# Attention scores on two halves of the array, with q and k transposed once

## The chip, the cores and the metric

The kernel is one layer of a streaming-encoder trunk. It runs on one core of a Trainium2 chip, in one launch. The metric is device time in microseconds, median of several runs.

The names used below: PE (TensorE) multiplies on a 128 x 128 array; "PEld" is its loading of weights (the stationary operand). DVE (VectorE), ACT (ScalarE) and POOL (GpSimd) work on rows of data; SP issues DMAs. A matmul contracts over the partitions of its two operands and writes to PSUM, of which this kernel's pool holds eight banks of 128 x 512 fp32.

## The reference, cut to what matters

```python
B_HEADS, B_HD, CHUNK, B_LEFT_CHUNKS = 8, 64, 64, 8      # SEQ = 1024, D_MODEL = 1024

def band_attention(q, k, v, qn_g, kn_g, rel_bias):
    """each chunk attends to itself and the previous 8 chunks"""
    qh = head_rms(q.reshape(bsz, seq, B_HEADS, B_HD), qn_g)
    kh = head_rms(k.reshape(bsz, seq, B_HEADS, B_HD), kn_g)
    ...
    scores = jnp.einsum('bnqhd,bnkhd->bnhqk', qc, kb) * (B_HD ** -0.5)
    scores = jnp.where(valid, scores + bias, -1e30)
    probs = jax.nn.softmax(scores, axis=-1)
    o = jnp.einsum('bnhqk,bnkhd->bnqhd', probs, vb)

def reference(...):
    h = rmsnorm(x, norm_mix_g)
    qa, fa, ia, ga, qb, kb, vb, gate_a, gate_b = jnp.split(h @ w_in, split_at, axis=-1)
    oa = hgrn2_mixer(qa, fa, ia, ga, ...)
    ob = band_attention(qb, kb, vb, ...)
    merged = sigmoid(gate_a) * (oa @ w_branch_a) + sigmoid(gate_b) * (ob @ w_branch_b)
    x = x + merged @ w_out
    ...     # then a SwiGLU feed-forward and a gated projection of p, each with its own rmsnorm
```

The change concerns the line of `scores`: per head, 128 queries at a time against up to 640 keys (five blocks of 128), over 64 channels.

## The kernel before

The kernel splits an fp32 operand into a high part rounded to fp32r and a residual ("hi" and "lo"), and computes hi x hi + hi x lo + lo x hi, each product in fp32r. The large products do so over 128 partitions.

The program runs in stages: the input projections (to 300 us of the profile), the recurrence `hgrn_mix` with further projections woven in (to about 432 us), the attention (432 to about 638 us), and then the branches, the output projection, the feed-forward and the last projection. Each engine executes its own queue in the order in which the Python code emits instructions. The helpers `self.V`, `self.A`, `self.mul`, `self.tr` and `self.load` pin that order on DVE, ACT, PE and SP; for that reason most instructions carry the line of the helper in the profile: L72 (DVE, ACT, POOL), L102 (matmul), L105 (transpose), L142 (the cast of a loaded weight to its high part).

**The attention stage.** `attention` walks through 32 steps. A step is a pair of heads and a block of 128 queries; two pairs alternate over the eight blocks (steps 0 to 15), then the two others do (16 to 31). In step n, in this order, with "feed" being a generator of other work for PE:

1. `stage(n-1, 1)`: DVE finishes the softmax of head 1 of the step before (reciprocal, scaling).
2. a feed call: two chunks of a projection, six 512-column products (in the first 28 steps `attn_in`, which makes q and k of the other head pairs; then the gates).
3. `scores(n, 0)`: head 0's score products, and DVE's reductions that add the bias and find the row maximum.
4. the first part of `attn_stack(n+1)`: transposes of the next q and k, and ACT's copies out of PSUM.
5. `scores(n, 1)`, then the rest of `attn_stack(n+1)` on DVE (the residuals).
6. in odd steps `attn_pv` of two earlier steps: probabilities times v, 40 records on PE, the two heads on the two column halves of the array.
7. `attn_pt(n-1, 1)`: five transposes of head 1's probabilities, copied out by ACT and DVE.
8. a second feed call.
9. `stage(n, 0)`, `stage(n, 1)`: ACT's exponentials; `attn_pt(n-1, 0)`; ACT's scaling of head 0; one queued residual split of weights on DVE (`rest`).

**The stack.** A head has 64 channels, half of the partitions. `attn_in` writes each head's q and k twice side by side (tile qk, the axis `two`), so that one transpose gives a 128-partition tile with the 64 channels twice. Of q the upper copy holds the high part and the lower copy the residual (`lo = qs[64:128, :]`); of k, `k1` holds the high part in both halves and `k2` the residual. Two products then give the sum: q with k1 (hi x hi + lo x hi) and q with k2. That takes four transposes and, per head, two products over 128 partitions; scores wider than 512 columns are cut in two parts, one PSUM bank each (384 + 256 columns for five key blocks). The tiles are named in the profile by role: m are small tiles (qk, qs, s, pt, bias, statistics), s are 128 x 1024 slots (k1, k2, v, activations), pm is PSUM, wh, wl and wr are a weight's high part, residual and raw load.

Of the kernel before, what the change touches and what calls it, by code (L numbers as in the profile page):

```python
# [22 lines left out]
HALF = 512  # L23
# [21 lines left out]
def f32(ap):  # L45
    return ap.bitcast(F32)
# [28 lines left out]
class Trunk:  # L75
# [526 lines left out]
                    self.nc.scalar.activation(self.v[p][:, b * P:b * P + P], ps[:, p * P:p * P + P], AF.Copy, scale=self.r[:, b:b + 1])  # L602

    def attn_setup(self):
        self.k1 = [self.slot(F32R) for _ in range(4)]
        self.k2 = [self.slot(F32R, late=i > 1) for i in range(4)]
        self.qs = {}

    def attn_in(self):

        nc = self.nc
        late = []

        def scale():
            two, b, ps, ss = late.pop(0)
            for i in range(2):
                qk = self.small(HALF, tag="qk")
                self.V.tensor_tensor(
                    qk[:, :].rearrange("p (a two d) -> p a two d", two=2, d=64),
                    ps[:, i * 256:i * 256 + 256].rearrange("p (a d) -> p a d", d=64).unsqueeze(2).to_broadcast([P, 4, 2, 64]),  # L620
                    ss[:, 4 * i:4 * i + 4].unsqueeze(2).unsqueeze(3).to_broadcast([P, 4, 2, 64]), ALU.mult)
# [24 lines left out]
    def attn_stack(self, pair, b):  # L646

        qk = self.qk.pop((pair, b))
        ps = self.mm()
        for a in range(4):  # L650
            self.tr(ps[:, a * P:a * P + P], qk[:, a * P:a * P + P], self.eye)
        t = slice(b * P, b * P + P)
        gk = self.cols[:, C_GK:C_GK + 1]
        k1, k2 = [k[pair % 2 * 2:pair % 2 * 2 + 2] for k in (self.k1, self.k2)]
        qs = self.small(256, F32R, tag="qs")
        self.qs[pair, b] = [qs[:, h * P:h * P + P] for h in range(2)]
        ksrc = [ps[:, 256 + h * P:256 + h * P + P] for h in range(2)]
        qsrc = ps[:, 0:256]
        self.A.activation(k1[0][:, t], ksrc[0], AF.Copy, scale=gk)
        self.A.activation(qs, qsrc, AF.Copy, scale=self.gq8[:, 0:1])  # L660
        self.A.activation(k1[1][:, t], ksrc[1], AF.Copy, scale=gk)
        yield
        lo = qs[64:128, :]
        for h in range(2):
            self.V.scalar_tensor_tensor(k2[h][:, t], ksrc[h], gk, f32(k1[h][:, t]), ALU.mult, ALU.subtract)
            if h == 0:
                self.V.scalar_tensor_tensor(lo, qsrc[64:128, :], self.gq8[64:128, 0:1], f32(lo), ALU.mult, ALU.subtract)

    def attn_scores(self, pair, b, h):

# [4 lines left out]
        bias = self.bias[pair, h]  # L675
        q = self.qs[pair, b][h]
        k1, k2 = [k[pair % 2 * 2 + h] for k in (self.k1, self.k2)]
        s = self.small(640, tag="s")
        mx = self.small(2, tag="mx2")
        last = None  # L680
        for i, (lo, hi) in enumerate(((0, na), (na, cols))):
            if hi == lo:
                continue
            ps = self.mm()
            n = hi - lo
            self.mul(ps[:, :n], q, k1[:, k0 + lo:k0 + hi], start=True, stop=False)
            self.mul(ps[:, :n], q, k2[:, k0 + lo:k0 + hi], start=False, stop=True)
            init = 3.0e38 if last is None else last
            self.V.tensor_tensor_reduce(s[:, lo:hi], ps[:, :n], bias[:, 640 - cols + lo:640 - cols + hi], -1.0, init, ALU.add, ALU.min, mx[:, i:i + 1])
            last = mx[:, i:i + 1]  # L690
        yield s, nb
        den = self.small(1, tag="den")
        self.A.activation(s[:, :cols], s[:, :cols], AF.Exp, bias=last, scale=-1.0, accum_out=den)
        yield
        self.V.reciprocal(den, den)
        if h == 0:
            self.A.activation(s[:, :cols], s[:, :cols], AF.Copy, scale=den)
        else:
            self.V.tensor_scalar(s[:, :cols], s[:, :cols], den, None, ALU.mult)

    def attn_pt(self, s, nb):
        pt = self.small(640, tag="pt")
# [19 lines left out]
    def attention(self):  # L722
# [17 lines left out]
        def scores(n, h):  # L740
            stages = self.attn_scores(*steps[n], h)
            sc[n, h] = (*next(stages), stages)

        def stage(n, h):
            if 0 <= n < whole:
# [19 lines left out]
        for n in range(whole + 2):  # L765
# [1340 lines left out]
MIXER = {"s": 3, "pt": 4, "bias": 4, "qk": 4, "qs": 2, "sq": 1, "state": 2}  # L2106


class Small:
# [140 lines left out]
```

## Time and profile before

| what | value |
|---|---|
| median of 3 runs | 1547.46 us (1546.5 to 1548.7) |
| the profiled execution | 1549.86 us, its span 1548.0 us |
| PE busy in the span | 1520.7 us (98%) |
| DVE, ACT, POOL busy | 1127.2, 670.7, 626.7 us |
| attention stage, 432 to 638 us: PE, DVE, ACT busy | 199.9, 158.8, 147.8 of 206.0 us |
| granted TensorE clock | 1.00 |

How the profile's lines are read: a row of a group names line, engine, operation, out<-in by the tiles' names, shapes, and xcount; then the busy time in us, the mean of one in ns, and the engine's idle time just before them with what ended it. A row of the timeline begins with start and duration in us; alike neighbours are merged into one row with their count. The shape 128*64 128x128 of a PE row means weights of 128 rows and 64 columns, and an output of 128 columns. Matmuls are pipelined: a record's duration is longer than the time for which it holds up the next one, so costs on PE are taken from start to start. The chain of waits follows the work that ended last back from the end.

### The profile page before, as it was taken

Reading aid. Unit: us, or ns where it says so; the run is one execution under the profiler, and the core shown is the slowest. Engines: PE = TensorE matmul, PEld = TensorE weight load, DVE = VectorE, ACT = ScalarE, POOL = GpSimd, SP = SyncE. Lnnn points to the kernel's source line nnn. Section 1 sums busy time; section 2 is a strip of 40 time slices with the busy share of each in tenths; the row PEclk is TensorE's granted clock in tenths of the full one; section 3 lists DMA queues with packets and bytes.
Section 4 is the critical chain, followed back from the end, with each engine's and each line's share of the span. In section 5 each row is a group of like instructions: output and inputs, shape, how many; then the busy total and the mean of one; then the engine's idle time right before and its main releaser. Section 6 shows DMA issues by size and latency. Waiting matters only on the chain.

```text
span 1548.0 us, 20662 instructions
## 1 busy us (share of the span) xinstructions
PE 1520.7 (98%) x7664; PEld 1266.2 (82%) x7664; DVE 1127.2 (73%) x1645; ACT 670.7 (43%) x1136; POOL 626.7 (40%) x349
## 2 busy tenths in 40 slices
PE   8999999999999999999999999999999999999998
PEld 6888888878788888788888788888888888888886
DVE  5787774776777778446888877777777767656678
ACT  6633333433377677421567222222222234456552
POOL 4233333010333222245212656665555545445546
PEclk9999999999999999999999999999999999999999
DMA  5544444898433443767346244443233288785425
GB/s 201 195 164 143 143 150 154 270 325 258 145 82 69 111 75 73 294 178 230 102 158 216 91 119 125 128 124 111 104 110 101 101 303 305 273 282 188 130 96 203
DMA packets 97044, 256.56 MB, mean 166 GB/s; under 512 B 10032, under 2 KB 14896, under 8 KB 96432
## 3 DMA queue, kind: packets, MB, share of 16 engines
q1 hardware_dynamic: 90400, 239.51, 45.0%
q0 software_dynamic: 6400, 15.73, 6.2%
q8 instruction: 60, 0.98, 0.3%
q14 instruction: 40, 0.33, 0.1%
q10 hardware_dynamic: 144, 0.02, 0.0%
HBM read 193.08 MB, written 93.59 MB: 185 GB/s over the span
## 4 chain that ended last, share of the span: by engine, by line
PE 89%; DVE 6%; ACT 2%; DMA 1%; issue 1%; POOL 0%; SPq 0%; DVEq 0%; ACTq 0%; POOLq 0%
PE pm L102 86%; DVE s L72 4%; PE pm L105 3%; DVE m L72 1%; ACT m L72 0%; ACT wh L142 0%; DMA s<-in_x 0%; DMA wr<-in_qk 0%; DMA wr<-in_fm 0%; DVE q L72 0%; ACT s L72 0%; DVE wl L72 0%; DMA wr<-in_wv 0%; DVE s L337 0%; DVE t L72 0%
## 5 line engine op out<-in xcount | busy, mean ns | idle before, releaser
L102 PE MATMUL pm<-s,whi 128*128 128x512 f32 x1792 | 552.4, 389 | 0.6 <-DVE t L72 0.6
L102 PE MATMUL pm<-s,wh 128*128 128x512 f32 (+1 forms) x1584 | 492.5, 392 | 7.0 <-ACT wh L142 5.2
L102 PEld LDWEIGHTS pm<-s,whi 128*128 128x128 f32 x1792 | 336.0, 188 | 71.5 <-DVE t L72 1.7
L102 PEld LDWEIGHTS pm<-s,wh 128*128 128x128 f32 x1584 | 295.6, 188 | 69.9 <-ACT wh L142 5.2
L102 PE MATMUL pm<-s,wlo 128*128 128x512 f32 x896 | 348.6, 389 | 0.0
L72 DVE TENSOR_TENSOR s<-s,s 128x512 f32<-128x512 f32 (+3 forms) x236 | 285.5, 1238 | 61.2 <-ACT s L72 47.7
L102 PE MATMUL pm<-s,wl 128*128 128x512 f32 x792 | 308.7, 390 | 0.5 <-POOL wl L150 0.5
L150 POOL TENSOR_TENSOR wl<-wr,wh 128x1024 fp32r<-128x1024 f32 (+2 forms) x72 | 175.3, 2440 | 222.5 <-ACT wh L142 222.4
L72 DVE TENSOR_TENSOR t<-pm,t 128x512 f32<-128x512 f32 x158 | 108.8, 689 | 132.9 <-PE pm L102 105.6
L142 ACT CAST wh<-wr 128x1024 fp32r<-128x1024 f32 (+2 forms) x106 | 106.5, 1005 | 208.4 <-PE pm L102 92.1
L102 PEld LDWEIGHTS pm<-s,wlo 128*128 128x128 f32 x896 | 168.2, 188 | 34.8
L102 PE MATMUL pm<-wh,s 128*128 128x512 f32 x512 | 180.0, 407 | 0.0
L102 PEld LDWEIGHTS pm<-s,wl 128*128 128x128 f32 x792 | 149.2, 188 | 32.0 <-POOL wl L150 1.2
L72 POOL TENSOR_TENSOR wlo<-wr,whi 128x512 fp32r<-128x512 f32 (+1 forms) x63 | 132.3, 2106 | 68.2 <-ACT whi L72 59.2
L72 POOL TENSOR_TENSOR wlo<-q,whi 128x512 fp32r<-128x512 f32 x62 | 100.0, 1614 | 139.7 <-ACT whi L72 75.5
L72 POOL TENSOR_TENSOR m<-m,mhalf 128x8 f32<-128x8 f32 (+1 forms) x24 | 35.0, 1459 | 229.1 <-DVE m L72 229.1
L72 ACT CAST s<-s 128x1024 fp32r<-128x1024 f32 (+1 forms) x94 | 90.4, 981 | 61.9 <-DVE s L72 31.6
L72 ACT CAST whi<-q 128x512 fp32r<-128x512 f32 (+1 forms) x93 | 70.5, 758 | 107.3 <-PE pm L102 84.6
L102 PEld LDWEIGHTS pm<-wh,s 128*128 128x128 f32 x512 | 96.4, 188 | 18.5
L72 POOL TENSOR_TENSOR s<-t,rb 128x512 f32<-128x512 f32 x44 | 70.7, 1607 | 98.5 <-ACT t L72 96.1
L102 PE MATMUL pm<-wl,s 128*128 128x512 f32 x256 | 99.9, 390 | 0.0
L72 ACT ACTIVATE t<-s 128x512 f32<-128x512 f32 x44 | 27.8, 633 | 159.3 <-DVE s L72 155.3
(147 smaller groups left out, 1835.3 us busy)
## 6 DMA issues: line engine op xcount, KB each, us to landing
s<-d SPq DMA_DIRECT2D x81, 512.0 KB, 6.2
d<-s SPq DMA_DIRECT2D x87, 256.0 KB, 2.4
wr<-d SPq DMA_DIRECT2D x36, 512.0 KB, 3.7
d<-s SPq DMA_DIRECT2D x32, 512.0 KB, 4.4
d<-t SPq DMA_DIRECT2D x46, 256.0 KB, 2.3
wr<-in_sg SPq DMA_DIRECT2D x22, 512.0 KB, 3.9
wr<-in_su SPq DMA_DIRECT2D x22, 512.0 KB, 4.9
s<-in_x SPq DMA_DIRECT2D x21, 512.0 KB, 8.6
```

The lines of the kernel that those rows point to most:

```text
L72: return lambda *a, **k: self.trunk.order(op(*a, **k), self.key)
L102: return self.order(self.nc.tensor.matmul(*a, **k))
L105: return self.order(self.nc.tensor.transpose(*a, **k))
L142: self.nc.scalar.copy(hi[:, c], raw[:, c])
L150: rest.tensor_tensor(lo[:, c], raw[:, c], f32(hi[:, c]), ALU.subtract)
```

## The change

The two heads of a pair are no longer stacked. One transpose turns both heads' q (64 channels each, 128 together) and one both heads' k. `q1`, `k1` are the high parts and `q2`, `k2` the residuals, in tiles that hold head 0 in partitions 0 to 63 and head 1 in 64 to 127. Each head's scores are now three products over its own 64 partitions; the products of the two heads are written in turn, and each goes to the half of the array's rows on which its operands lie. They write to different PSUM banks.

Around it: `attn_in` writes q and k once (one DVE operation of 512 columns per block instead of two); the stack issues two ACT copies and two DVE residuals instead of three and three; both heads' score products stand together, ahead of the next step's stack; head 1's row of scores takes a slot of the pool late1; the squares of `attn_in` share the buffers of qk; and the second feed call moves from behind `attn_pt(n-1, 1)` to ahead of `attn_pv`.

```diff
     def attn_setup(self):
-        self.k1 = [self.slot(F32R) for _ in range(4)]
-        self.k2 = [self.slot(F32R, late=i > 1) for i in range(4)]
+        self.ks = [[self.slot(F32R) for _ in range(2)] for _ in range(2)]
...
         def scale():
             two, b, ps, ss = late.pop(0)
+            qk = self.small(HALF, tag="qk")
+            self.V.tensor_tensor(
+                qk[:, :].rearrange("p (a d) -> p a d", d=64), ps[:, :].rearrange("p (a d) -> p a d", d=64),
+                ss[:, :].unsqueeze(2).to_broadcast([P, 8, 64]), ALU.mult)
             for i in range(2):
-                qk = self.small(HALF, tag="qk")
-                self.V.tensor_tensor(
...
-                self.qk[2 * two + i, b] = qk
+                self.qk[2 * two + i, b] = qk[:, 256 * i:256 * i + 256]
...
-                sq = self.small(HALF, tag="sq")
+                sq = self.small(HALF, tag="qk")
...
     def attn_stack(self, pair, b):
-        for a in range(4):
+        for a in range(2):
             self.tr(ps[:, a * P:a * P + P], qk[:, a * P:a * P + P], self.eye)
...
+        k1, k2 = self.ks[pair % 2]
         qs = self.small(256, F32R, tag="qs")
-        self.A.activation(k1[0][:, t], ksrc[0], AF.Copy, scale=gk)
-        self.A.activation(qs, qsrc, AF.Copy, scale=self.gq8[:, 0:1])
-        self.A.activation(k1[1][:, t], ksrc[1], AF.Copy, scale=gk)
+        q1, q2 = self.qs[pair, b] = qs[:, :P], qs[:, P:]
+        self.A.activation(k1[:, t], ps[:, P:2 * P], AF.Copy, scale=gk)
+        self.A.activation(q1, ps[:, :P], AF.Copy, scale=self.gq8[:, 0:1])
         yield
-        lo = qs[64:128, :]
-        for h in range(2):
-            self.V.scalar_tensor_tensor(k2[h][:, t], ksrc[h], gk, f32(k1[h][:, t]), ALU.mult, ALU.subtract)
-            if h == 0:
-                self.V.scalar_tensor_tensor(lo, qsrc[64:128, :], self.gq8[64:128, 0:1], f32(lo), ALU.mult, ALU.subtract)
+        self.V.scalar_tensor_tensor(k2[:, t], ps[:, P:2 * P], gk, f32(k1[:, t]), ALU.mult, ALU.subtract)
+        self.V.scalar_tensor_tensor(q2, ps[:, :P], self.gq8[:, 0:1], f32(q1), ALU.mult, ALU.subtract)

-    def attn_scores(self, pair, b, h):
+    def attn_scores(self, pair, b):
...
-            self.mul(ps[:, :n], q, k1[:, k0 + lo:k0 + hi], start=True, stop=False)
-            self.mul(ps[:, :n], q, k2[:, k0 + lo:k0 + hi], start=False, stop=True)
+        banks = [[self.mm() for _ in parts] for _ in range(2)]
+        for i, (lo, hi) in enumerate(parts):
+            c = slice(k0 + lo, k0 + hi)
+            for j, (q, k) in enumerate(((q1, k1), (q1, k2), (q2, k1))):
+                for h in range(2):
+                    r = slice(64 * h, 64 * h + 64)
+                    self.mul(banks[h][i][:, :hi - lo], q[r, :], k[r, c], start=j == 0, stop=j == 2)
+
+        def softmax(h):
...
+            s = self.slot(late=True)[:, :640] if h else self.small(640, tag="s")
...
     def attention(self):
...
-                scores(n, 0)
-            st = stack(n + 1)
-            next(st, None)
-            if n < whole:
-                scores(n, 1)
-            drain(st)
+                scores(n)
+            drain(stack(n + 1))
+            next(feed, None)
             if n % 2:
                 pv(n - 3)
                 pv(n - 2)
             pt(n - 1, 1)
-            next(feed, None)
             stage(n, 0)
```

What this does to the queues, in one odd step with five key blocks. On PE, before, from the first feed call's last product to the start of `attn_pv` (s_3771 and s_3772 are the k1 tiles of the two heads, s_3775 and s_3776 their k2, m_4788 is the q tile qs, m_4815 the next qk, m_4752 the transposed probabilities, s_2891 is v):

```order
L102 MATMUL pm_4766<-wh_4659,s_185 128x512
L102 MATMUL pm_4852<-s_3771,m_4788 128x384
L102 MATMUL pm_4852<-s_3775,m_4788 128x384
L102 MATMUL pm_4856<-s_3771,m_4788 128x256
L102 MATMUL pm_4856<-s_3775,m_4788 128x256
L105 MATMUL pm_4860<-eye,m_4815 128x128 x4
L102 MATMUL pm_4871<-s_3772,m_4788 128x384
L102 MATMUL pm_4871<-s_3776,m_4788 128x384
L102 MATMUL pm_4875<-s_3772,m_4788 128x256
L102 MATMUL pm_4875<-s_3776,m_4788 128x256
L102 MATMUL pm_4882<-m_4752,s_2891 64x128
```

The same place after the change (s_3768 is k1 and s_3769 k2, both heads in each; pm_4811 and pm_4812 are head 0's banks, pm_4813 and pm_4814 head 1's; the rows of the third product, which name the same tiles as the first, and those of the second part but its first are left out):

```order
L102 MATMUL pm_4729<-wh_4622,s_185 128x512
L102 MATMUL pm_4811<-s_3768,m_4763 128x384
L102 MATMUL pm_4813<-s_3768,m_4763 128x384
L102 MATMUL pm_4811<-s_3769,m_4763 128x384
L102 MATMUL pm_4813<-s_3769,m_4763 128x384
...
L102 MATMUL pm_4812<-s_3768,m_4763 128x256
...
L105 MATMUL pm_4835<-eye,m_4768 128x128 x2
L102 MATMUL pm_4729<-wh_4666,s_192 128x512
...
L102 MATMUL pm_4855<-m_4715,s_2888 64x128
```

Twelve score products stand where eight stood, in pairs; two transposes where four stood; and a feed call (its first product is shown) is between the stack and `attn_pv`.

On ACT, before, in the step in which a weight's cast (L142) is the feed's (s_3857 and s_3913 are outputs of `attn_pv`, m_4720 is the transposed probabilities, m_4664 and m_4683 are the score rows whose exponentials are taken):

```order
L72 COPY s_3857<-pm_4696 128x128
L72 COPY s_3913<-pm_4708 128x128
L72 COPY m_4720<-pm_4721 128x384
L142 CAST wh_4737<-wr_4738 128x1024
L72 ACTIVATE m_4742<-pm_4562 128x512
L72 ACTIVATE m_4664,m_4748<-m_4664,m_4665 128x640
L72 ACTIVATE m_4683,m_4750<-m_4683,m_4684 128x640
```

And after the change:

```order
L142 CAST wh_4666<-wr_4667 128x1024
L72 ACTIVATE m_4671<-pm_4527 128x512
L72 COPY s_3844<-pm_4677 128x128
L72 COPY s_3896<-pm_4689 128x128
L72 COPY m_4701<-pm_4702 128x384
L72 ACTIVATE m_4643,m_4711<-m_4643,m_4644 128x640
L72 ACTIVATE s_4647,m_4713<-s_4647,m_4648 128x640
```

The feed's cast and its square now stand ahead of the copies of `attn_pv`'s outputs and of the probabilities.

More of the change, by code (lines that the diff above doesn't have):

```diff
@@ L615, in scale @@
             two, b, ps, ss = late.pop(0)
+            qk = self.small(HALF, tag="qk")
+            self.V.tensor_tensor(
+                qk[:, :].rearrange("p (a d) -> p a d", d=64), ps[:, :].rearrange("p (a d) -> p a d", d=64),
+                ss[:, :].unsqueeze(2).to_broadcast([P, 8, 64]), ALU.mult)
             for i in range(2):
-                qk = self.small(HALF, tag="qk")
-                self.V.tensor_tensor(
-                    qk[:, :].rearrange("p (a two d) -> p a two d", two=2, d=64),
-                    ps[:, i * 256:i * 256 + 256].rearrange("p (a d) -> p a d", d=64).unsqueeze(2).to_broadcast([P, 4, 2, 64]),
-                    ss[:, 4 * i:4 * i + 4].unsqueeze(2).unsqueeze(3).to_broadcast([P, 4, 2, 64]), ALU.mult)
-                self.qk[2 * two + i, b] = qk
+                self.qk[2 * two + i, b] = qk[:, 256 * i:256 * i + 256]
         for two in range(2):
@@ L653, in attn_stack @@
         gk = self.cols[:, C_GK:C_GK + 1]
-        k1, k2 = [k[pair % 2 * 2:pair % 2 * 2 + 2] for k in (self.k1, self.k2)]
+        k1, k2 = self.ks[pair % 2]
         qs = self.small(256, F32R, tag="qs")
-        self.qs[pair, b] = [qs[:, h * P:h * P + P] for h in range(2)]
-        ksrc = [ps[:, 256 + h * P:256 + h * P + P] for h in range(2)]
-        qsrc = ps[:, 0:256]
-        self.A.activation(k1[0][:, t], ksrc[0], AF.Copy, scale=gk)
-        self.A.activation(qs, qsrc, AF.Copy, scale=self.gq8[:, 0:1])
-        self.A.activation(k1[1][:, t], ksrc[1], AF.Copy, scale=gk)
-        yield
-        lo = qs[64:128, :]
-        for h in range(2):
-            self.V.scalar_tensor_tensor(k2[h][:, t], ksrc[h], gk, f32(k1[h][:, t]), ALU.mult, ALU.subtract)
-            if h == 0:
-                self.V.scalar_tensor_tensor(lo, qsrc[64:128, :], self.gq8[64:128, 0:1], f32(lo), ALU.mult, ALU.subtract)
-    def attn_scores(self, pair, b, h):
+        q1, q2 = self.qs[pair, b] = qs[:, :P], qs[:, P:]
+        self.A.activation(k1[:, t], ps[:, P:2 * P], AF.Copy, scale=gk)
+        self.A.activation(q1, ps[:, :P], AF.Copy, scale=self.gq8[:, 0:1])
+        yield
+        self.V.scalar_tensor_tensor(k2[:, t], ps[:, P:2 * P], gk, f32(k1[:, t]), ALU.mult, ALU.subtract)
+        self.V.scalar_tensor_tensor(q2, ps[:, :P], self.gq8[:, 0:1], f32(q1), ALU.mult, ALU.subtract)
+    def attn_scores(self, pair, b):
         nb = min(b + 1, 5)
@@ L674, in attn_scores @@
         na = {1: 1, 2: 2, 3: 3, 4: 2, 5: 3}[nb] * P
[L675 to L685, printed above, removed]
-            self.mul(ps[:, :n], q, k1[:, k0 + lo:k0 + hi], start=True, stop=False)
-            self.mul(ps[:, :n], q, k2[:, k0 + lo:k0 + hi], start=False, stop=True)
-            init = 3.0e38 if last is None else last
-            self.V.tensor_tensor_reduce(s[:, lo:hi], ps[:, :n], bias[:, 640 - cols + lo:640 - cols + hi], -1.0, init, ALU.add, ALU.min, mx[:, i:i + 1])
-            last = mx[:, i:i + 1]
@@ L691, in attn_scores @@
[L691 to L699, printed above, removed]
+        q1, q2 = self.qs.pop((pair, b))
+        k1, k2 = self.ks[pair % 2]
+        parts = [(lo, hi) for lo, hi in ((0, na), (na, cols)) if hi > lo]
@@ new lines, in attn_scores @@
+        banks = [[self.mm() for _ in parts] for _ in range(2)]
[6 more added lines that the diff above has]
+        def softmax(h):
+            bias = self.bias[pair, h]
+            s = self.slot(late=True)[:, :640] if h else self.small(640, tag="s")
+            mx = self.small(2, tag="mx2")
+            last = None
+            for i, (lo, hi) in enumerate(parts):
+                init = 3.0e38 if last is None else last
+                self.V.tensor_tensor_reduce(
+                    s[:, lo:hi], banks[h][i][:, :hi - lo], bias[:, 640 - cols + lo:640 - cols + hi], -1.0, init, ALU.add, ALU.min, mx[:, i:i + 1])
+                last = mx[:, i:i + 1]
+            yield s, nb
+            den = self.small(1, tag="den")
+            self.A.activation(s[:, :cols], s[:, :cols], AF.Exp, bias=last, scale=-1.0, accum_out=den)
+            yield
+            self.V.reciprocal(den, den)
+            if h == 0:
+                self.A.activation(s[:, :cols], s[:, :cols], AF.Copy, scale=den)
+            else:
+                self.V.tensor_scalar(s[:, :cols], s[:, :cols], den, None, ALU.mult)
@@ L701, in attn_pt @@
+        return [softmax(h) for h in range(2)]
     def attn_pt(self, s, nb):
@@ L738, in stack, with scores @@
             return self.attn_stack(p, b)
-        def scores(n, h):
-            stages = self.attn_scores(*steps[n], h)
-            sc[n, h] = (*next(stages), stages)
+        def scores(n):
+            for h, stages in enumerate(self.attn_scores(*steps[n])):
+                sc[n, h] = (*next(stages), stages)
         def stage(n, h):
@@ L2105 @@
 FFN = {"q1024": 1, "q512": 3, "raw": 2, "tmp": 8}
-MIXER = {"s": 3, "pt": 4, "bias": 4, "qk": 4, "qs": 2, "sq": 1, "state": 2}
+MIXER = {"s": 3, "pt": 4, "bias": 4, "qk": 4, "qs": 2, "state": 2}
 class Small:
```

## The prediction

> **What bounds the kernel now.** I read the page first, then the stretches of the attention stage, the groups inside it, PE's rows in order of time, and last the chain of waits.
>
> ```profile
> PE 1520.7 (98%) x7664; PEld 1266.2 (82%) x7664; DVE 1127.2 (73%) x1645; ACT 670.7 (43%) x1136; POOL 626.7 (40%) x349
> PE 89%; DVE 6%; ACT 2%; DMA 1%; issue 1%; POOL 0%; SPq 0%; DVEq 0%; ACTq 0%; POOLq 0%
> ```
>
> PE is busy 98% of the span and is 89% of the chain that ended last. The attention stage, from 432 to 638 us, looks the same:
>
> ```profile
> core 0: us, PE busy (x) PEld busy (x) DVE busy (x) ACT busy (x) POOL busy (x), PEclk, DMA share, GB/s
> 432.00:638.00 206.00, 199.89 (x1486) 173.10 (x1485) 158.80 (x510) 147.75 (x381) 56.91 (x38) 1.00 0.41 96
> ```
>
> PE 97%, DVE 77%, ACT 72%, granted clock 1.00. So a ns saved or added on PE here is a ns of the end, unless a wait swallows it. What one step costs PE is read from one step, n=15, and the start of the next (five key blocks; start, time, engine, out<-in, count). A record lasts longer than its turn on the array, so I use start to start:
>
> ```profile
> 521.31 0.76 PE L102 MATMUL pm<-s,m 128*128 128x384 f32 x4
> 521.91 0.60 PE L105 MATMUL pm<-eye,m 128*128 128x128 f32 x4
> 522.26 0.84 PE L102 MATMUL pm<-s,m 128*128 128x384 f32 x4
> 523.03 2.40 PE L102 MATMUL pm<-m,s 128*64 128x128 f32 x40
> 525.37 0.77 PE L105 MATMUL pm<-eye,m 128*128 128x128 f32 x5
> 525.89 0.47 PE L102 MATMUL pm<-wh,s 128*128 128x512 f32 x1
> 527.36 0.71 PE L105 MATMUL pm<-eye,m 128*128 128x128 f32 x5
> 527.82 0.47 PE L102 MATMUL pm<-wh,s 128*128 128x512 f32 x1
> ```
>
> In order: the scores of head 0, the stack's transposes, the scores of head 1, the probabilities times v (attn_pv, two heads on the two column halves of the array), and the transposes of the probabilities.
>
> **The change, part by part.**
>
> *Transposes, four to two per step.* 32 steps lose 64 of them.
>
> ```profile
> 508.59 0.44 PE pm L105 x4
> ```
>
> That is 0.11 us each on the chain, so 64 x 0.11 = **-7.0 us**.
>
> *Score products, two per head to three, two heads at once.* Head 0 above streams 2 x (384 + 256) = 1280 columns from 521.31 to 521.91: 0.60 us, or 0.469 ns a column. The stage streams 80 x 384 + 112 x 256 + 16 x 128 = 61440 columns (the first two groups are the second and third row below, the rest the four steps with a single block):
>
> ```profile
> L105 PE MATMUL pm<-eye,m 128*128 128x128 f32 x376 | 57.9, 276 | 3.8 <-DVE m L72 3.8
> L102 PE MATMUL pm<-s,m 128*128 128x384 f32 x80 | 22.1, 357 | 0.0
> L102 PE MATMUL pm<-s,m 128*128 128x256 f32 x112 | 21.9, 289 | 2.3 <-DVE m L72 2.3
> L102 PE MATMUL pm<-m,s 128*64 128x128 f32 x480 | 29.7, 276 | 0.0
> ```
>
> 61440 x 0.469 ns = 28.8 us now. Afterwards each head streams three products instead of two, 92160 columns together. If the two heads run at once PE pays for 46080: 21.6 us, and some 0.6 us more because in the four one-block steps (three pairs each) a load of weights is longer than 128 columns. If they run one after the other it is 43.2 us. No product on part of the rows is in this trace; the nearest row is attn_pv, on part of the columns. Its 40 records take 523.03 to 525.37, 2.34 us; at 0.11 us each, as the transposes of the same 128x128 size, they would take 4.4 us in turn and 2.2 us in pairs. They run in pairs, and both ends stand: 22.2 us if rows pair as columns do, 43.2 us if they don't. I take pairs, the nearest row: 22.2 - 28.8 = **-6.6 us** (the other end: +14.4).
>
> *Changes of the array's mode.* Every step now leaves the full array for two row halves and comes back. The trace has the like around attn_pv. Going in: head 1's scores start at 522.26 and attn_pv at 523.03, 0.77 us for what took head 0 0.60; 0.08 of the difference was handed over by the transposes ahead (four in 0.35 instead of 0.44), so 0.09 is a wait. Within attn_pv: 2.34 - 20 pairs x 0.11 = 0.16, the first bare weight load and the wait at the way out. Coming back: five transposes take 525.37 to 525.89, 0.52, against 527.36 to 527.82, 0.46: 0.06 for their bare weight load. One round trip: 0.09 + 0.16 + 0.06 = 0.31 us. The scores' weights are fp32r, whose bare load is dearer; the last attn_pv goes back into such products:
>
> ```profile
> 631.16 2.40 PE L102 MATMUL pm<-m,s 128*64 128x128 f32 x40
> 633.50 0.72 PE L102 MATMUL pm<-s,wh 128*128 128x512 f32 x2
> 634.06 0.40 PE L102 MATMUL pm<-s,wl 128*128 128x512 f32 x1
> 634.30 0.62 PE L102 MATMUL pm<-s,wh 128*128 128x512 f32 x2
> 634.76 0.39 PE L102 MATMUL pm<-s,wl 128*128 128x512 f32 x1
> ```
>
> Two products take 0.56 (633.50 to 634.06) against 0.46 (634.30 to 634.76): 0.10 instead of 0.06, so a round trip for the scores is 0.31 + 0.05 = 0.36 us. All 32 steps make one, none shared with attn_pv's, since a feed call stands between: 32 x 0.36 = **+11.5 us**. The ends are 0 (halving rows costs nothing) and 32 x 0.6, were both ways to pay two fp32r loads in turn: +19.
>
> *Feed moved ahead of attn_pv and the transposes of head 1's probabilities.* The same instructions, earlier in five queues. On PE its six products (525.89 to 527.36 above less the 0.08, 1.39 us) now stand between the scores and whatever waits for the softmax; they cover PE's waits of this kind:
>
> ```profile
> 529.84 0.42 PE L102 MATMUL pm<-s,m 128*128 128x128 f32 x2
> 530.80 0.74 PE L105 MATMUL pm<-eye,m 128*128 128x128 f32 x5 [0.55 <-DVE m L72]
> 624.01 0.40 PE L102 MATMUL pm<-s,wl 128*128 128x512 f32 x1
> 627.16 0.74 PE L105 MATMUL pm<-eye,m 128*128 128x128 f32 x5 [2.76 <-DVE m L72]
> ```
>
> The first has head 1's probability transposes right behind the scores, waiting for DVE's normalisation: it starts 0.96 us after the products, of which about 0.2 is their own time, so some 0.75 go. The second waits for DVE, which sits in one residual split of weights:
>
> ```profile
> 623.51 2.85 DVE L72 TENSOR_TENSOR wl<-wr,wh 128x512 fp32r<-128x512 f32 x1
> 626.47 0.55 DVE L72 TENSOR_SCALAR m<-m,m 128x640 f32<-128x640 f32 x1
> ```
>
> The cover shortens it by 1.39 of its 2.76. The third long wait is a load's:
>
> ```profile
> 490.29 0.95 ACT wh L142
> 491.31 2.39 POOL wl L72
> 493.71 5.34 DMA wr<-in_qk
> 499.14 1.05 ACT wh L142
> ```
>
> ACT's cast waits for a load that waits for POOL's split of the cast before. In ACT's queue the earlier cast stands now ahead of a probability copy (0.48, row below) and has a k copy (0.36) less in front of it, so the load lands up to 0.8 us earlier; but ACT, blocked, now holds attn_pv's copies and head 1's probability copy too, which PE's next scores need for their banks. I take 0.4 off. Sum: -0.75 - 1.39 - 0.4 = **-2.5 us**. Ends: -5, if all waits of the stage that DVE ends go (PE's 3.8 before transposes and 2.3 before products, in the group rows above, less 1 that the load keeps), and +2, if the load's block costs a wait for banks of the same size as the 2.3 again. SP and POOL issue the same instructions in the same order, so the weight loads, the bias tables' loads and POOL's powers move past nothing in their own queues.
>
> *DVE and ACT.* The first five rows shrink:
>
> ```profile
> L72 ACT ACTIVATE s<-pm,cols 128x128 fp32r<-128x128 f32 x64 | 23.2, 363 | 3.0 <-PE pm L105 2.2
> L72 DVE SCALAR_TENSOR_TENSOR s<-pm,cols,s 128x128 fp32r<-128x128 f32 x64 | 22.4, 349 | 1.8 <-ACT s L72 0.7
> L72 DVE TENSOR_TENSOR m<-pm,m 128x512 f32<-128x512 f32 x30 | 19.2, 679 | 0.0
> L72 DVE SCALAR_TENSOR_TENSOR m<-pm,ones,m 64x256 fp32r<-64x256 f32 x32 | 15.7, 491 | 0.5
> L72 ACT ACTIVATE m<-pm,ones 128x256 fp32r<-128x256 f32 x32 | 14.9, 467 | 0.0
> L72 ACT COPY m<-pm 128x384 f32<-128x384 f32 x48 | 22.9, 477 | 6.4 <-PE pm L105 6.3
> L72 DVE CUSTOM_DVE_ANT_0 m<-pm,m 128x384 f32<-128x384 f32 x40 | 22.1, 553 | 16.8 <-PE pm L105 16.7
> L72 DVE CUSTOM_DVE_ANT_0 m<-pm,m,m 128x256 f32<-128x256 f32 x40 | 19.4, 484 | 3.6
> ```
>
> ACT loses 32 x 0.36 and 32 x (0.47 - 0.36), 15 us; DVE loses 32 x 0.35, 32 x (0.49 - 0.35) and 15 x 0.68, 26 us. Both hide under PE, so I count nothing. They are slack for the new order, in which DVE's four score reductions wait until the first part of both heads is through and q2 and k2 stand behind all four: 2 x 0.55 + 2 x 0.48 = 2.1 us of reductions (last two rows) and 2 x 0.35 for the two, 2.8 us, against the 4.1 that PE has until the next scores in a step without attn_pv (two feeds, 2.8, and twelve transposes, 1.3). If that cover went, each of the 32 steps would pay what is missing. Four banks are taken at once instead of two, but each step still takes the same number of the eight. The squares of attn_in share the four buffers of qk, of which each block again takes two, and head 1's score row moves into two buffers that held k; both cost nothing for the same reason, PE's cover.
>
> **Sum.** -7.0 - 6.6 + 11.5 - 2.5 = -4.6 us. The profiled execution took 1549.86 us (span 1548.0); that gives 1545.3. The runs' median, 1547.46, lies 2.4 lower, and the prediction is made for it: 1542.9.
>
> **Rivals.** A: *the two row halves run one after the other* (slower). Then the scores cost +14.4 instead of -6.6: 1542.9 + 21.0 = 1563.9. For it: nothing in the trace runs on half the rows. Against: the column halves pair. It decides from the pair's own price: with 1542.9 - 1547.5 = -4.6, a pair that takes 21% more than one product (4.6 of 22.2) brings no gain.
>
> B: *pairs, but dearer ones.* In attn_pv two loads of 0.05 fit under one product, so it can't show whether loads pair. Two fp32r loads of 0.10 in turn would give 0.2 us a pair; 156 pairs (3 x 20, 3 x 28, 3 x 4) make 31.2 instead of 22.2: +9.0, 1551.9. Milder: pairs at 1.3 of one product, 28.9, +6.7, 1549.6, no change or just slower. The Trainium skill ("TensorE: Matmul & The Clock Gate", Part 3, measured speedup) gives 3.07 for four row tiles of 32, 77% of the ideal; as an estimate from that, two tiles reach 1.54, a pair 1.3 of one product. No run here shows it; attn_pv's pairs at 1.0 speak against it.
>
> C: *halving the rows needs no change of mode.* Then the 11.5 us aren't paid: 1531.4. Against: both column modes pay at each change. The Trainium skill ("TensorEngine Tiling (Array Packing)", Key Properties) says that any change of tiling mode drains the array, by which C is out; the 0.31 us agree for columns, and no run here shows it for rows.
>
> D: *new waits eat the gain*: the banks and the blocked ACT above, +2 to +7 on the sum: 1545 to 1550.
>
> **How the numbers follow.** A measurement of this kernel can't tell less than about 0.2%, 3.1 us, from no change. The forecast has 0.53, its own range 1539 to 1547 (the pair's and the round trip's rounding, the waits' ends); about 0.40 of it is faster, 0.13 within. A 0.13, slower. B 0.14, half within and half slower. C 0.10, faster. D 0.10, mostly within. Together: faster 0.50, same 0.28, slower 0.22. The range takes in C at its low end and B at its high end and leaves out A: 1531 to 1556.
>
> **What would show it.** Right: the stage's transposes by 64 fewer; score records of 64 rows whose second head starts a few ns after the first, pairs at 0.18 (384 columns) and 0.12 (256); about 0.09 and 0.10 of idle around each group; no wait before head 1's probability transposes at the change from the first two head pairs to the next. Wrong: the second head's product a full product's time behind the first (A), pairs above 0.2 at 256 columns (B), no gap at the first score product (C), or waits of PE on DVE or ACT before the score products (D).

## The result, and the profile after

The changed kernel takes 1538.94 us (median of 4 runs, 1538.07 to 1539.85), the kernel before, beside it, 1547.01 us (1546.5 to 1548.7, 4 runs). The ratio is 0.9946, its 95% interval 0.9929 to 0.9963: 8.4 us faster, between 5.7 and 11.0. The forecast was 4.6 us faster. The profiled execution took 1538.07 us, its span 1536.3.

The page after: busy time by engine, and the chain that ended last by engine.

```profile
PE 1515.4 (99%) x7704; PEld 1248.4 (81%) x7704; DVE 1102.7 (72%) x1597; ACT 660.7 (43%) x1104; POOL 630.1 (41%) x349
PE 91%; DVE 5%; issue 1%; ACT 1%; DMA 1%; POOL 0%; SPq 0%; ACTq 0%; DVEq 0%; POOLq 0%
```

The stretch of the attention stage, which now ends some 10 us earlier, 2 of them for a wait of 2.06 us ahead of the stage, at 340.8 us, that this execution does not have (columns as in the prediction's row of 432 to 638 us):

```profile
432.00:626.00 194.00, 193.20 (x1511) 153.66 (x1509) 135.69 (x461) 137.34 (x348) 56.70 (x38) 1.00 0.42 100
```

PE is still the bound, at the same granted clock, and executes 40 instructions more (7664 before): 104 score products more, 64 transposes fewer. In the stage it is busy 193.2 of 194 us; before it was idle 6.1 of 206. The groups of the stage that changed, with the idle time ahead of them:

```profile
L105 PE MATMUL pm<-eye,m 128*128 128x128 f32 x182 | 31.9, 282 | 0.0
L105 PE MATMUL pm<-eye,s 128*128 128x128 f32 x120 | 19.2, 280 | 0.0
L102 PE MATMUL pm<-s,m 64*128 64x384 f32 x120 | 15.8, 368 | 0.0
L102 PE MATMUL pm<-s,m 64*128 64x256 f32 x168 | 15.1, 289 | 0.8 <-DVE m L72 0.8
L102 PE MATMUL pm<-s,m 64*128 64x128 f32 x24 | 2.2, 289 | 0.0
```

The 3.8 us of idle ahead of the transposes are gone, and of the 2.3 ahead of the 256-column products 0.8 are left. PE in order of time around one step's scores:

```profile
514.61 0.39 PE L102 MATMUL pm<-wh,s 128*128 128x512 f32 x1
514.93 1.16 PE L102 MATMUL pm<-s,m 64*128 64x384 f32 x12
516.02 0.44 PE L105 MATMUL pm<-eye,m 128*128 128x128 f32 x2
516.21 0.48 PE L102 MATMUL pm<-wh,s 128*128 128x512 f32 x1
516.52 0.40 PE L102 MATMUL pm<-wl,s 128*128 128x512 f32 x1
```

Twelve products stand between 514.93 and 516.02, 1.09 us. Two stretches of the timeline of a few ns show that they run in pairs; the first row has all that is in flight at 514.94, the second all by 515.22.

```profile
514.93 0.44 PE L102 MATMUL pm<-s,m 64*128 64x384 f32 x2
514.93 0.61 PE L102 MATMUL pm<-s,m 64*128 64x384 f32 x4
```

The second head's record starts 3 to 4 ns behind the first's (514.930 and 514.933, 515.209 and 515.213); the later pairs follow every 0.17 to 0.18 us at 384 columns and every 0.12 at 256. That is the price of one full-array product of the same width. The round trip shows too: the last product ahead of the group takes 0.327 (the median of the 32 groups; 0.32 here, 514.61 to 514.93) instead of 0.231, so 0.096 going in; the group takes 1.088 where six pairs at 0.177 and 0.118 take 0.885, so 0.203 for the bare load and the way out; the first transpose takes 0.165 instead of 0.109, so 0.056. Together 0.355 us.

### The profile page after: what moved, and what is told of

The parts are those of the page before. It is cut to its first block, busy times and chain, and to the rows that moved or that the text cites. A ratio compares the mean times of both kernels' runs of the same rounds, so it can differ in the third digit from the quotient of the medians.

```text
span 1536.3 us, 20676 instructions
## 1 busy us (share of the span) xinstructions
PE 1515.4 (99%) x7704; PEld 1248.4 (81%) x7704; DVE 1102.7 (72%) x1597; ACT 660.7 (43%) x1104; POOL 630.1 (41%) x349
## 4 chain that ended last, share of the span: by engine, by line
PE 91%; DVE 5%; issue 1%; ACT 1%; DMA 1%; POOL 0%; SPq 0%; ACTq 0%; DVEq 0%; POOLq 0%
PE pm L102 88%; DVE s L72 4%; PE pm L105 3%; DVE m L72 0%; DMA s<-in_x 0%; ACT s L72 0%; DVE q L72 0%; POOL wl L72 0%; DMA wr<-in_qk 0%; ACT m L72 0%; DVE s L337 0%; ACT wh L142 0%; DVE wlo L72 0%; DVE s L234 0%; ACT t L72 0%
## 5 line engine op out<-in xcount | busy, mean ns | idle before, releaser
L142 ACT CAST wh<-wr 128x1024 fp32r<-128x1024 f32 (+2 forms) x106 | 106.5, 1006 | 213.6 <-PE pm L102 94.3
```

The costliest lines, as they stand in the source:

```text
L142: self.nc.scalar.copy(hi[:, c], raw[:, c])
```

## The experiments

All ratios are to the kernel before, measured on the same chip at the same time. The name in brackets behind a heading is the label by which later paragraphs and the table call the run.

**The kernel before, again** (before_again). No edit.

> The kernel before, unchanged, as a control. The trace after lacks three waits of PE that the trace before had: 2.06 us at 340.8, 2.3 us at 500.4 and 2.76 us at 624.0. Theory 1 (chance of meeting): the first and the third arise when a DVE operation starts just after one of POOL's weight splits (2.4 us) and is held until that ends (2.85 us instead of 0.69); whether they meet depends on when a load lands, so they come and go between executions of the same program. Then this second profile lacks at least one of the two, and its span lies nearer the median of the runs (span 1544 to 1546). Theory 2 (fixed by the order): the waits belong to the program's order; then this profile shows all three within 0.3 us of the first and a span of 1548. Time for both: 1546 to 1549, ratio 1.000 within 0.15%.

1548.91 us, ratio 1.0002 [0.9993, 1.0010]. The wait of 2.06 us at 340.8 us, outside the change, which the first profile had, is absent; those at 498, 500, 528 and 622 us are all there, the first with 1.8 instead of 2.3 us and with a stretch of 3.4 us at half the granted clock behind it, from 501.3 us on. So the waits in attention belong to the order, and the 2 us at 340.8 (most of the gap between the profiled execution and the median, which the prediction subtracted) come and go; the second profile of the changed kernel has them.

**The feed call alone** (feed_only), moved in the kernel before:

```diff
             drain(st)
+            next(feed, None)
             if n % 2:
...
             pt(n - 1, 1)
-            next(feed, None)
```

> The kernel before with one edit: the second feed call stands ahead of attn_pv and of head 1's probability transposes. Scores and transposes are as before. Theory 2 (the cover of the feed removes the attention's waits, some 6 us): -5 to -6 us, 1541 to 1542. Theory 1 (the cover removes only what it covers, 0.75 + 0.4 + 0.4 + up to 1.4, the rest of the missing waits are chance meetings of DVE and POOL): -2 to -3 us, 1544 to 1545. Rival (the moved feed gains nothing by itself): 1547 within 1.

1556.1 us, ratio 1.0048 [1.0036, 1.0060]: 7.4 us slower. What PE waited for in its attention stage (430 to 640 us; time, times, longest):

```profile
PE pm L105 <- DVE m L72: 3.7, 10, 1.1
PE pm L105 <- ACT s L72: 1.1, 2, 0.6
PE pm L102 <- DVE m L72: 0.4, 2, 0.2
```

The waits are many and short; their sum, 5.2 us, is even below the 6.1 of the kernel before, and so does not explain the time. From its timeline, one of each kind, on PE and on DVE:

```profile
480.07 0.82 PE L102 MATMUL pm<-s,m 128*128 128x384 f32 x4
481.00 0.66 PE L105 MATMUL pm<-eye,m 128*128 128x128 f32 x4
...
501.26 0.77 PE L105 MATMUL pm<-eye,m 128*128 128x128 f32 x5 [0.49 <-ACT s L72]
...
500.81 0.56 DVE L72 CUSTOM_DVE_ANT_0 m<-pm,m 128x384 f32<-128x384 f32 x1 [2.66 <-PE pm L105]
```

The stack's transposes start 0.93 us after head 0's products instead of 0.60 (521.31 to 521.91 in the prediction). Taken from start to start, the loss shows. Here and below, PE's lost time is what its products take beyond the median for the same place in the order (the same kinds of products ahead and behind) over the traces of all runs, where that is over 0.06 us. It is 14.0 us in the stage, against 6.6 before, and the difference is the 7.4 us: 4.4 in 12 places ahead of the stack's transposes, 4.1 in 11 places at or behind the probability transposes, 3.9 in 33 places ahead of or among the score products, and 1.6 in two other places. The last row is head 1's first reduction on DVE: it waits for transposes of the step before, because its row of scores shares the three buffers s. The move puts a feed call in front of these transposes.

**The change without the feed call's move** (rows_only). In the changed kernel the call goes back behind `pt(n - 1, 1)`.

> The changed kernel with the second feed call put back behind head 1's probability transposes: only the scores on row halves and the two transposes are new. The array's terms as the prediction priced them give -7.0 - 6.6 + 11.5 = -2.1 us, so 1545 if the waits stay (theory 2: the cover was needed for them), with PE waiting about 1 us before head 1's probability transposes in short steps. Theory 1: -2 to -5 us, 1542 to 1545, as the meetings of DVE and POOL move with any change of timing. Rival (DVE's and ACT's relief removes the waits): 1539 to 1540, as the full change.

1542.4 us, ratio 0.9958 [0.9945, 0.9970]: 6.5 us faster, where the array's terms were to give 2.1. So the move, a loss by itself, would add some 2 us in the changed kernel, though the intervals of the two ratios overlap.

**attn_pv directly behind the scores** (pv_next), ahead of the stack and the feed call:

```diff
                 scores(n)
-            drain(stack(n + 1))
-            next(feed, None)
             if n % 2:
                 pv(n - 3)
                 pv(n - 2)
+            drain(stack(n + 1))
+            next(feed, None)
```

> The changed kernel with attn_pv moved ahead of the stack and the feed, directly behind the score products, so that in the 16 odd steps the array goes from row halves to column halves without the full array between. If each change of mode costs what the trace shows (0.10 us wait at the way out and 0.055 us for the bare load of the transposes' weights saved per odd step), 16 x 0.155 = -2.5 us against the changed kernel: 1536.5. If a change between two divided modes costs more than one to the full array, or attn_pv waits here for its probabilities' copies, no gain: 1539 or more.

1537.59 us, ratio 0.9932 [0.9919, 0.9946]. That is 1.5 to 2.2 us below the change by the ratios, but the intervals overlap: the 2.5 us are neither shown nor excluded.

**The changed kernel, again** (after_again), beside the next three.

> The changed kernel, unchanged, beside the others of this call on the same chip. Ratio to before 0.994 to 0.995 (1540 to 1541 where before takes 1549). Its trace has no wait of PE above 0.3 us in the attention but one of about 1 us at 496, and its attention stage takes 189.5 us for the products of before's 199 to 200.

1537.74 us, ratio 0.9942 [0.9928, 0.9956]. In attention its profile has one wait of PE, of 0.9 us, as expected.

**Head 0's products, then head 1's** (rows_serial), instead of in turn:

```diff
-            for j, (q, k) in enumerate(((q1, k1), (q1, k2), (q2, k1))):
-                for h in range(2):
+            for h in range(2):
+                for j, (q, k) in enumerate(((q1, k1), (q1, k2), (q2, k1))):
```

> The changed kernel with the score products in another order: head 0's three products of a part first, then head 1's, instead of in turn. Nothing else differs. If the array runs two row halves at once only where neighbours in the queue lie on different halves, three of four changes of half still pair and the rest run alone: per step with two parts of 384 and 256 columns 5 x 0.175 + 4 x 0.117 = 1.34 us instead of 0.88; over all steps +12 us. If order doesn't matter (the array looks ahead): 0. If pairs gave nothing in the first place: 0 as well, and the records of the changed kernel's pairs would not start 3 ns apart, which they do.

1539.45 us, ratio 0.9944 [0.9930, 0.9959]: no loss. The same cuts of the timeline, at 515.04, 515.05, 515.32 and 515.33, and the whole group:

```profile
515.04 0.44 PE L102 MATMUL pm<-s,m 64*128 64x384 f32 x1
515.04 0.45 PE L102 MATMUL pm<-s,m 64*128 64x384 f32 x2
515.04 0.61 PE L102 MATMUL pm<-s,m 64*128 64x384 f32 x3
515.04 0.62 PE L102 MATMUL pm<-s,m 64*128 64x384 f32 x4
...
515.04 1.16 PE L102 MATMUL pm<-s,m 64*128 64x384 f32 x12
```

Records start in pairs still, 10 ns apart instead of 3 (515.037 and 515.047, 515.316 and 515.326), and the group takes 1.094 us instead of 1.088. Three 384-column products in a row would take over 0.5 us before the other half's first could start; a second record starts 10 ns behind. The rows do not name the head, but products on the same half follow each other every 0.17 us, so the second record must be of the other half. PE thus starts head 1's first product, fourth in the program, ahead of head 0's second. The Trainium skill ("TensorE: Matmul & The Clock Gate", Part 3, The mechanism) says that matmuls start and end strictly in program order; read so, this trace disagrees, for products on different halves of the rows.

**Twenty more round trips** (extra_mode). The stack's two transposes go between the first and second part of the scores, in the 20 steps that have two parts:

```diff
+            if between is not None and i == 0 and len(parts) == 2:
+                next(between, None)
```

> The changed kernel with the next stack's two transposes set between the first and the second part of the score products, in the 20 steps that have two parts: 20 more round trips between the row halves and the full array, all else the same. By the price of 0.36 us a round trip: +7.2 us. If the round trip's gaps are hidden elsewhere (PE waits for DVE anyway): 0 to +2.

1546.3 us, ratio 0.9989 [0.9980, 0.9997]: 8.5 us above the changed kernel beside it. PE in order of time in one step:

```profile
483.02 0.40 PE L102 MATMUL pm<-wh,s 128*128 128x512 f32 x1
483.35 0.79 PE L102 MATMUL pm<-s,m 64*128 64x384 f32 x6
484.07 0.44 PE L105 MATMUL pm<-eye,m 128*128 128x128 f32 x2
484.44 0.63 PE L102 MATMUL pm<-s,m 64*128 64x256 f32 x6
485.00 0.50 PE L102 MATMUL pm<-wh,s 128*128 128x512 f32 x1
```

The two transposes take 0.37 us (484.07 to 484.44), where two at 0.11 make 0.22, and the bare load and the way out are paid in both parts. Attention, waits taken out, is 7.3 us longer: 0.37 us for each round trip, the prediction's 0.36. (8.5 us / 20 is 0.43.)

**DVE's relief given back** (dve_back). k2 and q2 are computed twice.

> The changed kernel with both residuals of a step (k2 and q2) computed twice: 32 x 0.70 = 22 us of DVE work back, near the 26 us that the change took off; results are the same. Theory 3 (the moved feed call only pays because DVE was relieved: with DVE's old load the back-to-back transposes wait for DVE's copies, which is what made the kernel with the feed call alone 7 us slower): +4 to +9 us, with PE waiting for DVE in many steps. Rival (what matters is the order of PE's own products; DVE is slack at 72% busy): 0 to +1 us.

1538.04 us, ratio 0.9940 [0.9928, 0.9952]: no change, with DVE up by 17 us (the page's busy times):

```profile
PE 1516.8 (99%) x7704; PEld 1250.0 (81%) x7704; DVE 1119.7 (73%) x1661; ACT 661.0 (43%) x1104; POOL 628.8 (41%) x349
```

So the shorter DVE work isn't what lets the moved feed call pay. What remained was head 1's row of scores, which the prediction had put at nothing. Two kernels give it back its place in the three buffers s, with the moved call (after_s3) and without it (rows_s3):

```diff
-            s = self.slot(late=True)[:, :640] if h else self.small(640, tag="s")
+            s = self.small(640, tag="s")
```

> The changed kernel, but head 1's row of scores takes a buffer of the three named s again, as before the change, instead of a slot of late1. Theory 4 (the row's buffer is what makes the moved feed call pay): head 1's first reduction then waits for the transposes of head 1's probabilities of the step before, which now stand behind a feed call and attn_pv; DVE gets to k2, q2 and the probability copies later and PE waits for them as in feed_only, where attention cost 9.7 us more than before. The kernel loses at least 4 of its 10 us: 1542 to 1550 us, and DVE's waits for transposes before its reductions go from about 1 to 30 us or more. Theory 5 (feed_only lost because the stack stood between the two heads' products, so that k2 came late): nothing changes, 1538 us within 1.

> The changed kernel with the feed call put back behind the transposes of head 1's probabilities, and with head 1's row of scores in the three buffers named s: neither the moved feed call nor the own row. rows_only, with the own row, took 1542.4 us. Theory 4: the reduction waits for transposes that stand right behind the products (or behind attn_pv) as in before, where 28 us of such waits of DVE cost PE little; so 1542 to 1545, and the moved feed call is worth -4 with the own row and more than 0 without it. Theory 5: the own row is worth nothing in either place, 1542.4 within 1.

They took 1542.92 and 1546.85 us. With rows_only and the change they make a square. The last two columns are PE's lost time in attention, as above, and the part of it that falls into stretches at half the granted clock:

| kernel | own row | feed moved | ratio to before | PE's lost time, us | at half clock, us |
|---|---|---|---|---|---|
| before | no | no | 1 | 6.6 | 0 |
| feed_only | no | yes | 1.0048 [1.0036, 1.0060] | 14.0 | 0 |
| rows_s3 | no | no | 0.9975 [0.9964, 0.9985] | 8.7 | 3.1 |
| rows_only | yes | no | 0.9958 [0.9945, 0.9970] | 5.2 | 1.2 |
| after_s3 | no | yes | 0.9953 [0.9941, 0.9965] | 5.5 | 0 |
| the change | yes | yes | 0.9946 [0.9929, 0.9963] | 1.4 | 0 |

What PE waited for in the stage, in rows_s3:

```profile
PE pm L105 <- DVE m L72: 5.1, 4, 2.8
```

in rows_only:

```profile
PE pm L105 <- DVE m L72: 2.3, 1, 2.3
PE pm L105 <- DVE s L72: 0.9, 2, 0.5
```

in after_s3:

```profile
PE pm L105 <- DVE m L72: 1.2, 3, 0.6
PE pm L105 <- ACT s L72: 1.1, 2, 0.9
```

and in the changed kernel:

```profile
PE pm L102 <- DVE m L72: 0.8, 1, 0.8
```

The group of DVE's first reductions at 384 columns, in after_s3, shows what the shared row makes DVE wait for; the last column is the idle time ahead of it:

```profile
L72 DVE CUSTOM_DVE_ANT_0 m<-pm,m 128x384 f32<-128x384 f32 x40 | 22.2, 555 | 38.4 <-PE pm L105 38.3
```

Before it was 16.7 us for transposes, and in the changed kernel, in both heads' rows:

```profile
L72 DVE CUSTOM_DVE_ANT_0 m<-pm,m 128x384 f32<-128x384 f32 x20 | 11.1, 554 | 1.1 <-PE pm L102 0.8
L72 DVE CUSTOM_DVE_ANT_0 s<-pm,m 128x384 f32<-128x384 f32 x20 | 11.1, 553 | 0.0
```

By the traces, from rows_s3 on, the own row alone takes 3.5 us of lost time, the moved call alone 3.2, both together 7.3. The spans of the profiled executions differ in the same way, by 3.3, 2.4 and 7.2 us, and so do the ratios: -2.6, -3.4, and -4.5 to -5.1 us for both (0.9975 to 0.9946 and, in its second measurement, 0.9942). Each ratio is uncertain by some 2 us, so the times alone would not show the own row's share: its intervals overlap in both places.

Part of this is the clock. In rows_s3 PE's two longest waits (1.55 us, to 497.74, and 2.76 us, to 621.18) each have a stretch of some 3.4 us at half the granted clock behind them; the third number from the end of these rows is the mean clock, 0.57 over 4 us:

```profile
498.00:502.00 4.00, 3.63 (x13) 2.94 (x12) 3.44 (x13) 3.35 (x8) 2.00 (x2) 0.57 0.34 57
621.00:625.00 4.00, 3.82 (x14) 3.21 (x15) 0.46 (x2) 0.48 (x1) 0.00 (x0) 0.57 0.02 4
```

There the 512-column products follow every 0.43 us instead of 0.23. rows_only has one such stretch, at its wait of 2.3 us, and after_s3 and the change have none in the stage. Without it, the lost time of rows_s3, rows_only, after_s3 and the change is 5.6, 4.0, 5.5 and 1.4 us. So the moved call alone takes two long waits away, with the half clock behind them, but brings as much in short ones: 4.1 us in 11 places at the probability transposes, as in feed_only. The own row alone takes 1.6 us of waits, both together 4.2.

Neither theory held whole. The own row shortens the waits in either place, and with it the moved call's short waits are gone, as theory 4 has it; but the call gains without it too, by the clock, once both heads' products stand together. (rows_s3, at 1546.85 us, is slower than both theories had it.) What makes the call a loss in the kernel before is settled in part. The waits at the probability transposes are shown to be the shared row's, since they stand in after_s3 as well and are gone with the own row. The 8.3 us ahead of the stack's transposes and at the score products occur in this form only where the stack stands between the heads' products; no kernel changed that alone, so this cause is argued, not shown.

**POOL's splits in halves** (half_before, pv_half). DVE's 2.85 us in the prediction's row at 623.51 is an operation that takes 0.67 or 0.68 in the three other places of the stage. In that timeline stands POOL's row:

```profile
623.45 2.37 POOL L72 TENSOR_TENSOR wl<-wr,wh 128x1024 fp32r<-128x1024 f32 x1 [22.05 <-ACT wh L142]
```

and in the changed kernel's, POOL's split and DVE's:

```profile
612.99 2.40 POOL L72 TENSOR_TENSOR wl<-wr,wh 128x1024 fp32r<-128x1024 f32 x1 [21.73 <-ACT wh L142]
...
614.92 1.01 DVE L72 TENSOR_TENSOR wl<-wr,wh 128x512 fp32r<-128x512 f32 x1
```

Before, DVE starts 0.07 us after POOL's split, and ends 0.55 after it; in the changed kernel it starts 1.93 later, and ends 0.55 after it again. The DVE operation seems to be held until POOL's is through. To test that, POOL's splits that the order pins were issued as two of 512 columns, in the kernel before (half_before) and in pv_next (pv_half):

```diff
+            for x in range(a, b, HALF):
+                c = slice(x, min(b, x + HALF))
+                rest.tensor_tensor(lo[:, c], raw[:, c], f32(hi[:, c]), ALU.subtract)
+            return
```

> The kernel before; each of POOL's splits of 128x1024 that the order pins is issued as two of 128x512. Theory 2 (a DVE operation that starts beside POOL's split is held until the split ends): the DVE split at 624 us, 2.85 us in all profiles of before, is held only for what is left of half a split, 1.2 us or less on top of 0.69, and PE's wait of 2.75 there falls to 0.5 to 1.7; the kernel gains 1 to 3 us. Rival (the operation is long for another reason, as the load of its operands or its own form): it stays at 2.8 us and the time at no change, or 0.5 slower for more issues on POOL.

1546.64 us, ratio 0.9984 [0.9975, 0.9993]: 2.5 us faster, between 1.1 and 3.9. Its timeline at the place of the 2.76 us wait, on DVE, POOL and PE:

```profile
619.14 1.76 DVE L72 TENSOR_TENSOR wl<-wr,wh 128x512 fp32r<-128x512 f32 x1
620.82 0.15 DVE L72 RECIPROCAL m<-m 128x1 f32<-128x1 f32 x1
621.01 1.36 DVE L72 TENSOR_SCALAR m<-m,m 128x640 f32<-128x640 f32 x1
...
619.07 2.95 POOL L72 TENSOR_TENSOR wl<-wr,wh 128x512 fp32r<-128x512 f32 x2 [22.07 <-ACT wh L142]
...
622.51 0.74 PE L105 MATMUL pm<-eye,m 128*128 128x128 f32 x5 [2.48 <-DVE m L72]
```

DVE's split is held half as long (1.76 instead of 2.85), which shows the mechanism. But the second half then holds the scaling that PE waits for (1.36 instead of 0.55), so PE's wait here falls by 0.3 us only, against an expected fall of 1 to 2. The waits of 2.34 and 0.31 us that the first profile has at 503 us are 0.17 and 0.75 here, at 498 and 499 us.

> attn_pv right behind the scores (as in pv_next, 1537.6 us) and POOL's splits in halves: a version meant to be the best. If DVE is held by POOL's splits, PE's waits at 397 to 418 us (3.5 us together in every kernel so far) and at 614 us (0.8) shrink by a third to a half: 1535 to 1537. If not, 1537.6 within 1.

1537.13 us, ratio 0.9918 [0.9906, 0.9930], the fastest kernel of the case, though not told apart from pv_next. PE's waits at 397 to 418 us did not shrink (1.41, 0.75, 0.80 and 0.29 us, and a new one of 0.43), against the expectation; in attention, the one at 495 to 497 us went from 1.1 us in pv_next to 0.3, and that at 615 us from 0.8 to 0.6.

## Why the prediction was right or wrong

It was right in the sign, and in what each operation on the array costs, but low by nearly half in the sum: 4.6 of 8.4 us.

- **Transposes, -7.0: right.** 64 fewer, at 0.109 us each inside a group.
- **Score products, -6.6: right, -7.2.** Waits and changes of mode taken out, they went from 29.0 to 21.8 us (priced 28.8 and 22.2). Pairs cost what one product costs, so rivals A and B are out. Since the halves pair even when written one head after the other, the order in turn wasn't needed.
- **Change of mode, +11.5: right.** 0.355 us, 32 times; twenty more cost 0.37 us each. Rival C is out. The Trainium skill's rule ("TensorEngine Tiling (Array Packing)", Key Properties) that a change of mode drains the array agrees for row halves too.
- These three give -7.0 - 7.2 + 11.4 = -2.8 us (priced -2.1). rows_s3, the change without its two rearrangements, is 3.9 us faster than before, between 2.3 and 5.6. In the traces its stage, from the first score product to the last of attn_pv, is 1.6 us shorter with 2.1 us more lost time, which leaves -3.7 us for the array, 0.9 more than these terms.
- **Waits, -2.5: the step that failed.** PE's lost time in attention went from 6.6 to 1.4 us, -5.2; the idle time that the profile itself counts went from 6.1 to 0.8. That is about the -5 that the prediction gave as an end, for the case that all waits that DVE ends go. The -2.5 was the moved feed call's. By itself the call does not bring it: in the kernel before it costs 7.4 us, and from rows_s3 to after_s3 it changes the waits by 0.1 us and gains by the clock, which the prediction did not count; that this comes near 2.5 in size is luck. The failed step is the sentence that head 1's score row moves into two buffers and that this "cost nothing": it was read as a cost to be hidden, and not as the end of a wait. With the own row the call's short waits go too, and of the 5.5 us in after_s3 1.4 are left. The profile showed that wait: 16.7 us of DVE's idle ahead of the 384-column reductions, put down to transposes, in the last row but one of the prediction's last list of groups.
- "The cover shortens it by 1.39 of its 2.76": it took away all of it. What held DVE there was the moment at which it met POOL's split, and in the changed kernel the split comes first (612.99 against 614.92). The prediction quoted the row with 2.85 us and did not ask why it is four times the usual.
- "The third long wait is a load's" is true in part. In the changed kernel 0.80 of its 2.34 us is left, and it too is DVE held, in an operation on eight columns that takes 0.23 us elsewhere (the changed kernel's timeline):

```profile
497.02 0.61 PE L102 MATMUL pm<-s,m 64*128 64x256 f32 x5 [0.80 <-DVE m L72]
...
494.67 0.69 DVE L72 TENSOR_REDUCE m<-m 128x8 f32<-128x512 f32 x1 [2.19 <-ACT m L72]
495.39 1.25 DVE L72 TENSOR_SCALAR m<-m,m 128x8 f32<-128x8 f32 x1
...
494.22 2.39 POOL L72 TENSOR_TENSOR wl<-wr,wh 128x1024 fp32r<-128x1024 f32 x1 [0.45 <-ACT wh L142]
```

- **DVE and ACT, 0: right**, by dve_back. **Rival D** did not come in the changed kernel: there, no product or transpose of the stage waits for ACT.

Sum: -2.8 - 5.2 = -8.0 us, inside the measured 5.7 to 11.0.

## What to carry to other kernels

Price a change of tiling mode by reading three places of the trace (the last product before, the group, the first product after), and count how often it is paid: here it ate most of what the transposes and the shorter products gave. When a change gives a tile a buffer of its own, look for the wait of which the old shared buffer was the end, on whichever engine it stands, and count its removal as a term. A wait of the array can cost more than its length: look at the granted clock behind it. And when an elementwise operation in a row is several times its usual length, look at what the neighbouring engine began just before; moving or splitting either of them can be worth as much as the arithmetic that is saved (here 2.5 us in half_before, against the 2.8 of the array's terms).

## What the runs showed of the hardware

- A DVE operation that reads and writes SBUF can be held until POOL's 128x1024 split ends: 2.85 us instead of 0.68 (split), 1.25 instead of 0.23 (eight columns). Half as long a split holds it half as long. It isn't every operation: a reduction of 512 columns at 494.67, beside the same split, took its usual 0.69. The Trainium skill ("SBUF — State Buffer", SBUF: two separate sides) says that the two engines share ports under an exclusive lock for the whole instruction; the trace agrees, for the operations held.
- Products on two halves of the array's rows start 3 to 4 ns apart (the step at 514.93), and still pair when up to two products of the other half stand between them in the program (10 ns apart).
- All four stretches at half the granted clock in the attention stages of these traces (two in rows_s3, one each in rows_only and before_again) begin within 1.3 us of the end of a wait of PE of 1.5 to 2.8 us. Such a wait need not bring one: the first profile of the kernel before has none behind 2.3 and 2.8 us.
